# Order of the tap matmuls in a state-space mixer: by tile size instead of group by group

## The chip, the cores and the metric

The kernel runs on one core of one Trainium2 chip. The metric is the device time of one execution in microseconds (us). Three executions of the kernel before took 2615.53, 2616.75 and 2618.24 us; the median, 2616.75 us, is the time before.

## What is computed

Six layers work on x, 256 tokens of 1024 channels in float32. Layers of four kinds of mixer (Fourier, state-space, dilated attention, and a last block with a selective-state and a sparse-attention part) alternate with feed-forward layers (`ffn`). Only the second mixer, the state-space one, is touched. Cut to what matters:

```python
lam_bar = exp(lam * dt)                               # [2 directions, 64 groups, 64 states], complex
b_bar = ((lam_bar - 1) / lam)[..., None] * b          # [.., 64 states, 16 channels]
h[t] = lam_bar * h[t-1] + b_bar @ u[t]                # a scan over 256 tokens, per group, both directions
y[t] = real(c @ h[t])                                 # 16 channels of each group
```

The kernel does this in chunks of 8 tokens. Within a chunk, the output takes the inputs of the same chunk through 16x16 matrices, the taps K_t = Re(C a^t B_bar) for t = -7..7. The taps depend on parameters only, not on x.

## The kernel before, in words

**Dense products.** Nearly all the time is dense products. Weights come in slabs of 128x1024 float32 (512 KB, `W._dma`, L157, on SyncE's queue into 4 buffers). ScalarE makes a rounded copy `whi` (L169), VectorE the remainder `wlo` (L170), into 4 buffers each; two slabs are split ahead of the one in use. `slab_step` issues 12 matmuls for a slab: four times the three products hi*hi, hi*lo and lo*hi (`product`, L307 to L309), with 512 moving columns each.

**Side work.** After every second group of three matmuls `S.tick()` lets the deferred tasks run that are due. So the order of every engine's instructions is fixed when the program is written; each engine takes its own in that order.

**The state-space parameters.** They are prepared while the first feed-forward layer runs. Each weight split calls `s5.run(RATE)`, which puts up small VectorE jobs (`product_jobs`: `first` L1453, `second` L1459 twice, `third` L1464) by a budget of 2.6 units a split. They form the table C a^t for a set of 4 groups in one half of the tile `s5set`. `store` sends that half to DRAM from GpSimd's queue (L1487) and defers `taps(m, ...)` by three ticks. There are 16 sets (m = 0..15); the work for set m+2 writes the half that set m used.

**Taps (L1541 to L1566).** For one set, two PSUM banks `fwd` and `bwd` are filled by small float32 matmuls (L1555). The array is addressed in tiles by `tile_position=(lo, 32 * q)`: q = 0..3 is the group in the set and the quadrant of 32 array columns; `lo` and the height give the array rows. Per part r (real, imaginary) and per q there are three matmuls: `bwd` on rows 64 to 127 (112 moving columns), `fwd` for t = 0 on all 128 rows (16 columns), and `fwd` for t > 0 on rows 0 to 63 (112 columns). That makes 24 matmuls a set; in the trace each shows as two passes, that is two weight loads and two matmuls. After them a matmul with the identity adds the skip term (L1558, two passes), ScalarE copies both banks out (L1563, L1564), and every second set goes to DRAM (L1566). The order of the loops is r, then q, then the three kinds.

**Other tiled matmuls of this kernel**, which the prediction reads as a comparison: `part` (L1752) issues 128-row, 32-column tiles over the four quadrants one after the other; `index_scores` (L907) issues 64-row tiles of all 128 columns for rows 0 and 64 in turn, into two banks; `spread` (L1619) issues 32-row transposes for four row positions in turn, into four banks; `trans` (L476) issues plain 128x128 transposes.

Of the kernel before, what the change touches and what calls it, by code (L numbers as in the profile page):

```python
# [72 lines left out]
class Sched:  # L73
    """Deferred pieces of work, emitted between the steps of the dense products."""
# [12 lines left out]
    def pipeline(self, n, stages, every, wait=0):  # L87
        """stages of (fn, lag): fn(i) at step i + lag; the tasks of the steps"""
        def step(s):
            def f():  # L90
                for fn, lag in sorted(stages, key=lambda x: -x[1]):
                    if 0 <= s - lag < n:
                        fn(s - lag)
            return f
        return self.pace([step(s) for s in range(n + stages[-1][1])], every, wait)

    def join(self, n, fn, delay):
        """defers fn at the n-th call"""
        left = [n]

        def arrive():
            left[0] -= 1
            if left[0] == 0:
                self.defer(fn, delay)
        return arrive
# [20 lines left out]
    def require_in(self, tasks, k):  # L126
        """the same for a task that may only be put up by another one"""
        while k in tasks and tasks[k] is None:
            self._run(self._next())
        if k in tasks:  # L130
            self.require(tasks[k])
# [6 lines left out]
class Weights:  # L138
    """The weight slabs of the whole program in the order of use: DMA, then the
    exact split w = hi + lo, both ahead of the products."""  # L140
# [45 lines left out]
    def split_ahead(self):  # L186
        """one more slab than the products need now"""
        if self.n_split < self.n_used + self.split_bufs:
            self._split()
# [10 lines left out]
class Pair:  # L200
    """An operand in its two exact parts."""
# [6 lines left out]
def tile_two_blocks(ctx: ExitStack, tc: tile.TileContext, A, out, upto=None, taps=None):  # L208
# [96 lines left out]
    def product(ps, lhs, rhs, start, stop):  # L305
        """ps += lhs^T rhs from the exact parts of both."""
        nc.tensor.matmul(ps, lhs.hi, rhs.hi, start=start, stop=False, skip_group_check=True)  # L307
        nc.tensor.matmul(ps, lhs.hi, rhs.lo, start=False, stop=False, skip_group_check=True)  # L308
        nc.tensor.matmul(ps, lhs.lo, rhs.hi, start=False, stop=stop, skip_group_check=True)  # L309

    def rsqrt_steps(v, n):
        """v^-1/2 by Newton's steps from the exponent's estimate: the result and what computes it"""
        y = small.tile([P, n], F32, tag=f"rs{n}", name="rsq")
        t = small.tile([P, n], F32, tag=f"rt{n}", name="rst")

        def estimate():
            nc.vector.tensor_scalar(t.bitcast(I32), v.bitcast(I32), 1, None, OP.logical_shift_right)
            nc.vector.tensor_scalar(y.bitcast(I32), t.bitcast(I32), -1.0, 1597463007.0, OP.mult, OP.add)

        def newton():  # L320
            nc.vector.tensor_tensor(t, y, y, OP.mult)
            nc.vector.scalar_tensor_tensor(t, t, -0.5, v, OP.mult, OP.mult)
            nc.vector.scalar_tensor_tensor(y, t, 1.5, y, OP.add, OP.mult)

        return y, (estimate, newton, newton, newton)
# [7 lines left out]
    class Normed:  # L333
        """x * gain, transposed and split, with the row scale apart."""
# [64 lines left out]
        def chunk_by_parity(self, kc, t):  # L399
            """128 tokens of one parity: the odd ones for t = 0"""  # L400
            S.require(self.tasks[kc // 4])
            s = slice(kc * T + 1 - t, (kc + 1) * T, 2)
            return Pair(self.hi[:, s], self.lo[:, s])
# [10 lines left out]
    def in_proj(xn, nblk, evict, src=None, after_head=None, bank=lambda b: acc()):  # L414
        """natural-layout blocks of 512 columns of (x gain) @ W, each handed to evict."""
        head = {}
        for b, s in order_in(nblk):
            if b not in head:
                head[b] = [bank(b) for _ in range(NT)]
            slab_step(head[b], src(b) if src else xn.chunk, 2 * s, W.take(), s == 0, s == 3)  # L420
            if s == 3:
                evict(b, head.pop(b))
                if b == 1 and after_head is not None:
                    after_head()

    def out_proj(src, nk, scale, xn):
        """x += scale * (y @ W); the halves of the next norm start as they end."""
        for h in range(2):
            ps = [acc() for _ in range(NT)]
            for s in range(nk // 2):  # L430
                slab_step(ps, src, 2 * s, W.take(), s == 0, s == nk // 2 - 1)
            for t in range(NT):
                xs = x[:, t, h * 512:(h + 1) * 512]
                nc.vector.scalar_tensor_tensor(xs, ps[t], scale, xs, OP.mult, OP.add)  # L434
            xn.half_ready(h)

    class Chunks:
        """A transposed operand [k, tokens] in two parts, 128 rows a chunk."""
# [86 lines left out]
    def bias_vectors():  # L525
        """The additive score term of every head by offset, in DRAM as [head, 512 | 256 | 256]:
        one group of heads per part, a large negative where the offset is not attended."""
# [23 lines left out]
    def backwards(ap):  # L551
        """[p, 256 tokens] read at 255 - t - 2 n for (t, n)"""
# [4 lines left out]
    def attention(xn, nxt):  # L557
# [16 lines left out]
        def unit_block(b):  # L574
            """block -> (half, unit or None, group)"""
# [190 lines left out]
    def sincos(ang, sin, cos, t):  # L766
        """sin and cos of ang; t is scratch of the same shape, ang is lost"""
# [10 lines left out]
    def rope_tables():  # L778
        """per rotated width n: cos [p, t, n] and (-sin, sin) [p, t, 2, n]"""
# [16 lines left out]
    def rope(v, t, first, n):  # L796
        """v [p, heads, width] rotated in place in its first 2n columns"""
# [13 lines left out]
    def transposed(src, widths=128):  # L811
        """[p, 128] tiles, one per entry of src, transposed side by side into one bank"""
# [5 lines left out]
    def mixer(xn, nxt, li):  # L818
# [76 lines left out]
        def index_scores(t, h0):  # L895
            """the scores of queries t, from heads h0 on as many as two banks hold"""
# [32 lines left out]
        def top_keys(i):  # L929
            """8 more of the 64 best keys of each query"""  # L930
# [81 lines left out]
        def steps():  # L1012
            """dt = softplus, and the running sum of dt a"""
# [59 lines left out]
        def similar():  # L1073
            """C B^T per group, causal, then the heads one by one"""
# [60 lines left out]
        def normalize(g):  # L1135
            """the gate and the norm of a group of 8 heads, then its four chunks of 128 channels"""
# [137 lines left out]
    class S5:  # L1274
        """The state-space mixer in chunks of 8 tokens: the groups' inputs of a chunk reach the state at its
        end (the other end for the backward direction) through B_bar a^k, the state runs over the 32 chunks,
        and a chunk's outputs take C a^k of the state before it and the taps K_t = Re(C a^t B_bar) of the
        tokens in it. Groups go in sets of 4 (one per partition quadrant), channels as (direction, state)."""
# [21 lines left out]
        def plan(self):  # L1300
# [128 lines left out]
            def sums(side, part):  # L1429
                """for products of x in three multiplications: x0 + x1 and y0 + y1, y0 - y1"""  # L1430
# [12 lines left out]
            def product_jobs(side, m):  # L1443
                """(q, r, (j, k)) of 4 groups: x times the conjugate of y for side c, times y for side b"""
# [96 lines left out]
        def taps(self, m, ct):  # L1541
            """K of a set of 4 groups to DRAM: columns are bwd t = 7..1, t = 0, fwd t = 1..7"""
# [3 lines left out]
            ct = ct.rearrange("p (q r k) -> p q r k", q=4, r=2)  # L1546
            for r in range(2):
                for q in range(4):
                    g = 4 * m + q
                    n = 16 if q == 3 else 32  # L1550
                    lhs = bb[:, r, g:g + n // 16].rearrange("p g k -> p (g k)")
                    for ps, at, lo, hi, rhs in ((bwd, 0, 64, 128, ct[64:, q, r, 16:]),
                                                (fwd, 0, 0, 128, c[:, r, g]),
                                                (fwd, 16, 0, 64, ct[:64, q, r, :112])):
                        nc.tensor.matmul(ps[32 * q:32 * q + n, at:at + rhs.shape[1]], lhs[lo:hi], rhs,  # L1555
                                         start=r == 0 and at == 0, stop=r == 1, skip_group_check=True,
                                         tile_position=(lo, 32 * q))
# [19 lines left out]
        def first_half(self, xn):  # L1577
            """the first half of the channels, without the row scale, while the products before go on"""
# [12 lines left out]
        def turn_in(self, xn, h, e):  # L1591
            """x to U's order [(j, p), chunk]: 4 pieces of 2 chunks of 128 channels each"""
# [42 lines left out]
        def mix(self, xn, nxt):  # L1635
# [44 lines left out]
            def place(k):  # L1680
                """the chunk ends of two sets, transposed, to the order of the steps"""
# [31 lines left out]
            def scan_ops(w):  # L1713
                """the steps of one half of the groups, op by op; each ends with the copies it lets go"""
# [88 lines left out]
        def outputs(self, b, ps, oT):  # L1803
            """the steps from the sums of two chunks of 128 channels to their part of the operand"""
# [233 lines left out]
```

## Time and profile before

| what | value |
| --- | --- |
| median of three executions | 2616.75 us |
| span of the profiled execution, first to last instruction | 2613.9 us |
| TensorE busy | 2529.4 us, 97% of the span, 13056 matmul passes |
| VectorE busy | 1617.6 us, 62% |
| ScalarE busy | 1338.9 us, 51% |
| stretch with the taps, 80 to 235 us: TensorE / VectorE / ScalarE busy | 155.0 / 98.0 / 48.9 us |
| share of L1555 in the chain of that stretch | 41.8% |

The execution that was profiled has no time of its own beside its span; the span is 2.85 us below the median. "PE" is TensorE's matmuls, "PEld" its weight loads, DVE is VectorE, ACT ScalarE, POOL GpSimd, SP SyncE. Shapes such as 64\*32 are the rows and columns of the array tile; 64x112 is partitions by moving columns. In the timelines neighbouring instructions of one line are merged: a row gives the start of the first, the time to the end of the last, and their number. A matmul's duration includes its way through the array, so durations of neighbours overlap.

### The profile page before, as it was taken

To read this page: it belongs to the slowest core of one execution; us is meant where nothing else is said; L and a number is where in the kernel's file an instruction comes from. 1 tells how busy PE (TensorE), PEld (TensorE's weight loads), DVE (VectorE), ACT (ScalarE), POOL (GpSimd) and SP (SyncE) were. 2 spreads that over 40 slices of the span, in tenths; PEclk is the share of its full clock that TensorE was granted. 3 is DMA by queue.
4 is the path that set the end of the run, shared out by engine and by line. 5 is a ranking of instruction groups with operands and counts; after the bars stand their busy time and mean duration, and the time that the engine had idled before them with its cause. 6 is when DMAs were issued, how large, how long until landed. Compare 5 with 4: busy or idle time off the path is not lost.

```text
span 2613.9 us, 34796 instructions
## 1 busy us (share of the span) xinstructions
PE 2529.4 (97%) x13056; PEld 2069.1 (79%) x13056; DVE 1617.6 (62%) x2870; ACT 1338.9 (51%) x2053; POOL 56.4 (2%) x98
## 2 busy tenths in 40 slices
PE   8999969999999999999999999899999999999998
PEld 6767747888778888888888888788888888778886
DVE  7757876555565556555555556776555555876654
ACT  5334565544455555444444445675444444676543
POOL 0000000000100100000000000000000000000000
PEclk9999989999999999999999999999999999999999
DMA  5545696555644525645555565545565655545554
GB/s 178 179 161 182 211 231 219 183 184 163 212 157 129 164 96 178 193 146 171 184 180 194 184 192 160 171 130 166 187 193 178 190 188 175 173 132 163 178 182 148
DMA packets 131945, 456.35 MB, mean 175 GB/s; under 512 B 14889, under 2 KB 23988, under 8 KB 129344
## 3 DMA queue, kind: packets, MB, share of 16 engines
q1 hardware_dynamic: 123616, 426.96, 51.4%
q0 software_dynamic: 7584, 26.51, 3.1%
q8 instruction: 103, 1.69, 0.3%
q10 hardware_dynamic: 576, 0.66, 0.1%
q14 instruction: 66, 0.54, 0.1%
HBM read 437.57 MB, written 16.50 MB: 174 GB/s over the span
## 4 chain that ended last, share of the span: by engine, by line
PE 59%; issue 32%; DVE 3%; DMA 3%; ACT 3%; POOL 0%; ACTq 0%; SPq 0%; DVEq 0%; POOLq 0%
PE acc L307 17%; PE acc L309 16%; PE acc L308 16%; PE aux L1555 2%; PE aux L815 1%; DMA local<-s_k 1%; PE aux L476 1%; DVE wlo L170 1%; ACT whi L169 1%; PE aux L674 1%; DMA csb<-cs_d 1%; PE aux L715 0%; DMA raw<-in_qkv_dram 0%; PE aux L381 0%; PE aux L1211 0%
## 5 line engine op out<-in xcount | busy, mean ns | idle before, releaser
L170 DVE TENSOR_TENSOR wlo<-raw,whi 128x1024 fp32r<-128x1024 f32 (+1 forms) x774 | 922.9, 1219 | 420.8 <-ACT whi L169 419.3
L169 ACT ACTIVATE whi<-raw 128x1024 fp32r<-128x1024 f32 (+1 forms) x774 | 790.3, 1054 | 266.1 <-PE acc L309 234.3
L307 PE MATMUL acc<-whi,xhi 128*128 128x512 f32 (+1 forms) x2104 | 845.8, 402 | 5.6 <-ACT whi L169 3.1
L308 PE MATMUL acc<-wlo,xhi 128*128 128x512 f32 (+1 forms) x2104 | 822.2, 391 | 5.4 <-DVE wlo L170 5.1
L309 PE MATMUL acc<-whi,xlo 128*128 128x512 f32 (+1 forms) x2104 | 823.4, 391 | 0.0
L307 PEld LDWEIGHTS acc<-whi,xhi 128*128 128x128 f32 x2104 | 398.4, 189 | 89.1 <-issue 6.2
L308 PEld LDWEIGHTS acc<-wlo,xhi 128*128 128x128 f32 x2104 | 398.9, 190 | 83.4 <-DVE wlo L170 8.1
L309 PEld LDWEIGHTS acc<-whi,xlo 128*128 128x128 f32 x2104 | 397.7, 189 | 84.9
L307 PE MATMUL acc<-whi,yhi 128*128 128x512 f32 x976 | 387.4, 397 | 2.1 <-ACT yhi L451 1.1
L308 PE MATMUL acc<-wlo,yhi 128*128 128x512 f32 x976 | 381.5, 391 | 3.2 <-DVE wlo L170 3.2
L309 PE MATMUL acc<-whi,ylo 128*128 128x512 f32 x976 | 381.6, 391 | 0.0
L468 ACT ACTIVATE silu<-acc,rsq 128x256 f32<-128x256 f32 x176 | 83.4, 474 | 289.0 <-PE acc L309 289.0
L469 DVE SCALAR_TENSOR_TENSOR hb<-acc,rsq,silu 128x256 f32<-128x256 f32 x176 | 84.7, 483 | 228.5 <-ACT silu L468 228.4
L308 PEld LDWEIGHTS acc<-wlo,yhi 128*128 128x128 f32 x976 | 183.9, 188 | 40.9 <-DVE wlo L170 4.4
L307 PEld LDWEIGHTS acc<-whi,yhi 128*128 128x128 f32 x976 | 183.8, 188 | 40.4 <-ACT yhi L741 1.6
L309 PEld LDWEIGHTS acc<-whi,ylo 128*128 128x128 f32 x976 | 183.6, 188 | 39.9 <-DVE ylo L452 0.7
L451 ACT ACTIVATE yhi<-aux 128x512 fp32r<-128x512 f32 (+1 forms) x104 | 58.7, 564 | 192.6 <-PE aux L476 190.1
L452 DVE TENSOR_TENSOR ylo<-aux,yhi 128x512 fp32r<-128x512 f32 (+1 forms) x104 | 67.5, 649 | 105.8 <-ACT yhi L451 105.5
L390 ACT ACTIVATE xhi<-aux,gains 128x256 fp32r<-128x256 f32 x104 | 40.7, 475 | 86.3 <-PE aux L381 86.3
L392 DVE SCALAR_TENSOR_TENSOR xlo<-aux,gains,xhi 128x256 fp32r<-128x256 f32 x104 | 43.1, 478 | 50.6 <-ACT xhi L390 50.6
L434 DVE SCALAR_TENSOR_TENSOR x<-acc,x 128x512 f32<-128x512 f32 x52 | 35.7, 692 | 56.3 <-PE acc L309 56.3
L1555 PE MATMUL aux<-s5set,s5bb 64*32 64x112 f32 (+1 forms) x512 | 54.5, 266 | 0.0
(359 smaller groups left out, 1942.0 us busy)
## 6 DMA issues: line engine op xcount, KB each, us to landing
raw<-in_ffn_in_dram SPq DMA_DIRECT2D x352, 512.0 KB, 4.2
raw<-in_ffn_out_dram SPq DMA_DIRECT2D x176, 512.0 KB, 4.1
raw<-in_mix_in_dram SPq DMA_DIRECT2D x96, 512.0 KB, 3.6
raw<-in_qkv_dram SPq DMA_DIRECT2D x72, 512.0 KB, 4.3
raw<-in_mix_out_dram SPq DMA_DIRECT2D x32, 512.0 KB, 3.6
raw<-in_fnet_w_out_dram SPq DMA_DIRECT2D x16, 512.0 KB, 3.9
s_ct<-s5set POOLq DMA_DIRECT2D x16, 512.0 KB, 3.8
raw<-in_s_glu_dram SPq DMA_DIRECT2D x16, 512.0 KB, 4.5
```

The lines of the kernel that those rows point to most:

```text
L169: self.nc.scalar.activation(hi[:, :w], r, AF.Copy)
L170: self.nc.vector.tensor_tensor(lo[:, :w], r, hi[:, :w].bitcast(F32), OP.subtract)
L307: nc.tensor.matmul(ps, lhs.hi, rhs.hi, start=start, stop=False, skip_group_check=True)
L308: nc.tensor.matmul(ps, lhs.hi, rhs.lo, start=False, stop=False, skip_group_check=True)
L309: nc.tensor.matmul(ps, lhs.lo, rhs.hi, start=False, stop=stop, skip_group_check=True)
L390: nc.scalar.activation(hi, p, AF.Copy, scale=g)
L392: nc.vector.scalar_tensor_tensor(lo, p, g, hi.bitcast(F32), OP.mult, OP.subtract)
L451: nc.scalar.activation(p.hi, ps, AF.Copy)
L452: nc.vector.tensor_tensor(p.lo, ps, p.hi.bitcast(F32), OP.subtract)
L468: nc.scalar.activation(s, ps[t][:, :256], AF.Silu, scale=r)
L469: nc.vector.scalar_tensor_tensor(hb[:, t * 256:(t + 1) * 256], ps[t][:, 256:], r, s, OP.mult, OP.mult)
L1555: nc.tensor.matmul(ps[32 * q:32 * q + n, at:at + rhs.shape[1]], lhs[lo:hi], rhs, start=r == 0 and at == 0, stop=r == 1, skip_group_check=True,
```

## The change

Inside `taps` the body of the innermost loop becomes a function `step`, and the calls of it are put in another order: first the eight 128-row matmuls of the set over r and q, then the sixteen 64-row ones, rows 64 to 127 and rows 0 to 63 in turn, over r and q. The matmuls, their operands, their tiles and their start and stop flags are the same, as is all that follows. Elsewhere the diff only takes out comment strings, which issue nothing.

```diff
+            def step(ps, at, r, q, lo, hi, rhs):
+                g = 4 * m + q
+                n = 16 if q == 3 else 32
+                lhs = bb[:, r, g:g + n // 16].rearrange("p g k -> p (g k)")
+                nc.tensor.matmul(ps[32 * q:32 * q + n, at:at + rhs.shape[1]], lhs[lo:hi], rhs,
+                                 start=r == 0 and at == 0, stop=r == 1, skip_group_check=True,
+                                 tile_position=(lo, 32 * q))
+
             for r in range(2):
                 for q in range(4):
-                    g = 4 * m + q
-                    n = 16 if q == 3 else 32
-                    lhs = bb[:, r, g:g + n // 16].rearrange("p g k -> p (g k)")
-                    for ps, at, lo, hi, rhs in ((bwd, 0, 64, 128, ct[64:, q, r, 16:]),
-                                                (fwd, 0, 0, 128, c[:, r, g]),
-                                                (fwd, 16, 0, 64, ct[:64, q, r, :112])):
-                        nc.tensor.matmul(ps[32 * q:32 * q + n, at:at + rhs.shape[1]], lhs[lo:hi], rhs,
-                                         start=r == 0 and at == 0, stop=r == 1, skip_group_check=True,
-                                         tile_position=(lo, 32 * q))
+                    step(fwd, 0, r, q, 0, 128, c[:, r, 4 * m + q])
+            for r in range(2):
+                for q in range(4):
+                    step(bwd, 0, r, q, 64, 128, ct[64:, q, r, 16:])
+                    step(fwd, 16, r, q, 0, 64, ct[:64, q, r, :112])
             nc.tensor.matmul(fwd[:112, :16], ident[:, :112], self.skip[:, m * 16:(m + 1) * 16],
                              start=False, stop=True, skip_group_check=True)
```

## Rows read from the trace of the kernel before

**Rows 1.** The page: span, and busy time of each engine.
```profile
span 2613.9 us, 34796 instructions
...
PE 2529.4 (97%) x13056; PEld 2069.1 (79%) x13056; DVE 1617.6 (62%) x2870; ACT 1338.9 (51%) x2053; POOL 56.4 (2%) x98
```

**Rows 2.** Busy time by stretch: the taps, the rest of the preparation, the mixer.
```profile
core 0: us, PE busy (x) PEld busy (x) DVE busy (x) ACT busy (x) POOL busy (x), PEclk, DMA share, GB/s
80.00:235.00 155.00, 155.00 (x1186) 107.86 (x1185) 98.02 (x120) 48.85 (x85) 14.16 (x24) 1.00 0.52 173
235.00:275.00 40.00, 40.00 (x204) 33.44 (x203) 36.83 (x46) 21.45 (x31) 4.88 (x10) 1.00 0.66 215
...
380.00:420.00 40.00, 26.18 (x373) 20.02 (x374) 23.54 (x104) 25.52 (x36) 1.58 (x3) 0.82 0.79 256
```

**Rows 3.** Chain of 80 to 235 us: start, length, engine and line.
```profile
by line: PE aux L1555 41.8%; PE acc L307 18.3%; PE acc L308 17.4%; PE acc L309 17.3%; PE aux L1558 3.1%; PE aux L476 2.3%
...
81.17 4.05 PE aux L1555 x46
...
85.84 0.23 PE acc L308
...
229.41 4.05 PE aux L1555 x46
```

**Rows 4.** Timeline of TensorE in one set of taps (start, length, instructions).
```profile
160.03 0.38 PE L1555 MATMUL aux<-s5set,s5bb 64*32 64x112 f32 x2
160.34 0.24 PE L1555 MATMUL aux<-s5c,s5bb 128*32 128x16 f32 x2
160.50 0.38 PE L1555 MATMUL aux<-s5set,s5bb 64*32 64x112 f32 x4
160.82 0.23 PE L1555 MATMUL aux<-s5c,s5bb 128*32 128x16 f32 x2
160.98 0.38 PE L1555 MATMUL aux<-s5set,s5bb 64*32 64x112 f32 x4
...
164.08 0.37 PE L1558 MATMUL aux<-s5skip,ident 128*112 128x16 f32 x2
```

**Rows 5.** Timeline of 160.81 to 160.83 us alone: the second passes.
```profile
160.62 0.26 PE L1555 MATMUL aux<-s5set,s5bb 64*32 64x112 f32 x2
```

**Rows 6.** Timeline of the quadrant matmuls of the mixer.
```profile
397.06 1.08 PE L1752 MATMUL acc<-ct,H 128*32 128x128 f32 x32 [1.41 <-DMA ct<-s_ct]
...
412.72 3.27 PE L1752 MATMUL acc<-local,H 128*32 128x128 f32 x112 [0.58 <-ACT H L1735]
```

**Rows 7.** Timeline of the two-row-half matmuls of the last block.
```profile
1630.93 1.14 PE L907 MATMUL aux<-kiT,qiT 64*128 64x256 f32 x8
```

**Rows 8.** Timeline of the transposes at four row positions.
```profile
356.41 0.69 PE L1619 MATMUL acc<-ident,hq 32*128 32x32 f32 x32
```

**Rows 9.** Chain of 88 to 89 us: four plain transposes of 128 columns.
```profile
88.37 0.44 PE aux L476 x4
```

**Rows 10.** Busy time and granted clock around rows 6 and rows 7.
```profile
397.05:398.20 1.15, 1.08 (x32) 0.81 (x32) 0.37 (x2) 1.12 (x3) 0.29 (x1) 1.00 0.96 399
1630.90:1632.00 1.10, 1.10 (x10) 0.70 (x9) 1.10 (x4) 0.00 (x0) 0.00 (x0) 1.00 0.84 331
```

**Rows 11.** Timeline of VectorE, 159 to 183 us: idle times in brackets.
```profile
165.75 1.23 DVE L170 TENSOR_TENSOR wlo<-raw,whi 128x1024 fp32r<-128x1024 f32 x1 [1.51 <-ACT whi L169]
...
175.06 0.48 DVE L469 SCALAR_TENSOR_TENSOR hb<-acc,rsq,silu 128x256 f32<-128x256 f32 x1 [3.89 <-ACT silu L468]
...
176.37 0.48 DVE L469 SCALAR_TENSOR_TENSOR hb<-acc,rsq,silu 128x256 f32<-128x256 f32 x1 [0.83 <-ACT silu L468]
177.32 1.22 DVE L170 TENSOR_TENSOR wlo<-raw,whi 128x1024 fp32r<-128x1024 f32 x1 [0.47 <-ACT whi L169]
```

**Rows 12.** Waits of 80 to 235 us: total us, times, longest.
```profile
ACT taps L1563 <- PE aux L1555: 69.7, 16, 6.6
DVE wlo L170 <- ACT whi L169: 32.1, 18, 4.4
```

## The prediction

> **What bounds the kernel now.** I read the page first, for the engine that fills the span: TensorE is busy 97% of 2613.9 us, VectorE 62% [rows 1]. That is an average, so next I cut the span where the changed line runs. Its 16 sets lie between 81.17 and 229.41 + 4.05 = 233.46 us [rows 3], and in 80 to 235 us TensorE is busy 155.0 of 155 us at full granted clock, VectorE 98.0, ScalarE 48.9, with the DMA engines half used [rows 2]. The chain of that stretch is TensorE alone: 41.8% of it is L1555, the rest dense products [rows 3]. So a microsecond taken from the taps is a microsecond of the kernel, as long as TensorE stays the last to be ready. One set holds the chain for 4.05 us, the first as the last [rows 3]; 16 x 4.05 = 64.8 us is all that there is to gain.
>
> Then I asked what those 4.05 us are. The timeline of a set shows a beat: four 64-row passes from 160.50, two 128-row passes from 160.82, and the next 64-row ones from 160.98 [rows 4]. That is 0.32 + 0.16 = 0.48 us per (r, q), eight times, 3.8 us, and the ends make 4.05. What streams in a beat is little. A plain pass of 128 columns takes 0.44 / 4 = 0.11 us [rows 9], so one of 112 columns takes 0.096. In the 0.32 us two tiles run side by side, two passes each: 0.19 us. The second passes start at 160.62 [rows 5], so they have streamed by 160.72, and yet the next tile size starts only at 160.82: 0.10 us in which the array empties. The same 0.10 out of the 128-row part's 0.16 leaves 0.06 for its two passes of 16 columns, 0.03 each, mostly their weight loads. So a set pays about 0.10 us sixteen times for a change of tile size, and lets at most two of its tiles work at once.
>
> **The change, part by part.** Removed: the alternation of tile sizes. A set now changes size once inside (128 to 64 rows), and once to the skip matmul, which it did before too. Added: nothing; 48 passes stay 48. Moved: order within one set on one engine's queue, so nothing is moved past a DMA, SP's or POOL's instructions. The wait for `s5set` moves from the first matmul to the ninth, which can only be earlier ready; no wait is added.
>
> *Part one, eight 128-row matmuls over four quadrants.* The trace has the like: L1752, 128 rows by 32 columns over the quadrants. 32 passes of 128 columns take 1.08 us there and 112 take 3.27 [rows 6], at full clock [rows 10]: with the last one's way through the array in it, 3.27 / 112 = 0.029 us a pass, against 0.11 alone [rows 9]. Four quadrants work at once, without loss. So part one is four rounds (two r, two passes) of about 0.03 us, 0.02 for the start of the other quadrants, and 0.10 to empty: 0.24 us. Bounds: 0.16, one old 128-row part; and 8 x 0.06 + 0.10 = 0.58, if quadrants didn't overlap. I take 0.24, since L1752 is the nearest row.
>
> *Part two, sixteen 64-row matmuls.* Eight tiles (four quadrants, two row halves). That both halves of one column strip work at once is shown by L907: 8 passes of 256 columns take 1.14 us to the end of the last [rows 7], at full clock [rows 10], where one after another at 0.22 each would need 1.76. Eight tiles at once are shown nowhere. If they all work together, it is four rounds of 0.096 us, 0.03 for the first weights, 0.05 for the start of the others, 0.10 to empty: 0.56 us. If only four do, it is eight rounds: 0.95. If only the pairs of the present order do, 16 rounds and 1.7. I take 0.56: quadrants and row halves are each free in the trace, and no row shows a limit on both.
>
> Sum: 0.24 + 0.56 = 0.80 us a set for 4.05. 16 x 3.25 = 52 us. The profiled execution's 2613.9 us would become 2561.9; the median lies 2.85 above that span, so 2616.75 - 52 = 2564.75, say 2565 us.
>
> *Is it kept?* Once TensorE needs only 155 - 52 = 103 us here, VectorE with 98.0 is next: 95%. What it waits for is ScalarE (wlo after whi, 32.1 us), and ScalarE in turn stands 69.7 us before the copies of the taps, that is, behind TensorE [rows 12]. So those waits shrink with the taps. Those that stay between two sets and the next two are 1.51, 0.83 and 0.47 us [rows 11]; they exist only while VectorE is early, and vanish when it is late. The weights are split two slabs ahead, 2 x 12 x 0.23 = 5.5 us of dense work [rows 3], which covers one late set. I therefore cost VectorE at nothing; without that cover see the fourth rival. ScalarE goes to 48.9 of 103, the DMA engines from 0.52 to 0.52 x 155 / 103 = 0.78, which the mixer's own stretch reaches too (0.79) [rows 2]. The next stretch, 235 to 275 us, is in TensorE's hands with VectorE at 92% [rows 2]; it starts from the last taps as before, so what is won stays won.
>
> **A rule against it.** In rows 6, passes on four quadrants of the same array rows follow each other at 0.029 us, so their weight loads are hidden. The Trainium skill ("TensorE: Matmul & The Clock Gate", Part 3, "The mechanism") says that a weight load overlaps with matmuls in flight only when its row group differs, which the quadrants of a half don't do. By that rule the passes of a half would follow each other; the fifth rival is priced for that mechanism, from rows. L1752 speaks against it.
>
> Also, 32 passes of 32 columns take 0.69 us elsewhere [rows 8], 0.022 each. The Trainium skill ("TensorEngine Tiling (Array Packing)", Performance Considerations, "Instruction Overhead") states some 60 cycles for each matmul however short; by that figure sixteen passes in line would make part one 16 x 0.025 + 0.10 = 0.50 us, an estimate from that page, and the time 4 us more. These passes are quicker, with their tail in it.
>
> **The rivals.**
> 1. *Half the tiles at once.* Rows 7 show two row halves, rows 6 four quadrants, no row eight tiles. Part two 0.95: set 1.19, gain 16 x 2.86 = 46 us: 2571.
> 2. *Feeding.* 96 weight loads and matmuls would leave the queue in 0.8 us. The longest run of small passes that I read, 112 in 3.27 us [rows 6], is 0.029 a pass, though streaming bounds it; 48 x 0.029 + 0.10 = 1.49, gain 16 x 2.56 = 41: 2576. Against it: the passes at 0.022 [rows 8].
> 3. *No effect.* The engine reorders passes over tiles already, or a later stage gives the gain back. Against it: the beat of rows 4 repeats through every set, and the later mixer waits follow program order. 2617.
> 4. *VectorE takes over.* If the waits of rows 11 (2.81 us per two sets) stay in full, two sets take 98.0 / 8 + 2.81 = 15.1 us against 12.9 for TensorE, so 2.2 x 8 = 17 us are lost: 2582. For it: 95% load. Against it: those waits go when it runs late.
> 5. *Loads in line.* Part one 16 x 0.03 + 0.10 = 0.58; part two, each half's 16 passes at 0.12 (0.03 load, 0.096 stream): 2.0. Gain 16 x 1.45 = 23: 2594.
> 6. *Slower: tiles next to each other that drain.* If going from one row half to the other in the same column strip empties the array, as a change of size does, each 64-row matmul costs what the lone first one does, 0.31 us (160.03 to 160.34) [rows 4]: 16 x 0.31 + 8 x 0.16 = 6.2 us a set, +2.2 x 16 = 35: 2652. It decides from 4.05 / 24 = 0.17 us a matmul. Against it: rows 7, where the halves alternate in one strip and overlap.
>
> **How the numbers follow.** Forecast 0.58; rivals 1 to 6: 0.12, 0.09, 0.04, 0.11, 0.03, 0.03. Faster by over 0.2% (5 us, about what three runs can tell from no change): forecast and rivals 1, 2, 4, 5, 0.93; within: 0.04; slower: 0.03. Low end: part one at 0.16 and no start costs in part two (0.51) make 0.67 a set, 54 us, 2563, and some us below for the mixer stage, whose granted clock of 0.82 [rows 2] depends on where its idle times fall: 2559. High end: rivals 1, 2 and 4 in: 2583. Left out: about 0.1 above, and little below.
>
> **What would show it.** In the profile after, a set from its first matmul to the skip matmul: 0.8 us (right), 1.2 (rival 1), 1.5 with gaps (rival 2), 2.6 (rival 5), over 4 (rival 6); and one change of tile size in it, not sixteen. TensorE busy through a stretch that is 52 us shorter; idle TensorE there, with wlo or `s5set` as releaser, would show rival 4. L1752's stretch should stay as long as it is. The prediction is wrong if the set shrinks and the stretch doesn't, or if the set stays over 1.6 us.

## The result, and the profile after

The kernel after takes 2569.4 us (median of 4 runs, 2566.44 to 2571.25) against 2616.49 us for the kernel before (4 runs beside it): ratio 0.9817, 95% interval 0.9802 to 0.9831, 47.1 us faster. The forecast was 2565 us, range 2559 to 2583. The execution that was profiled took 2569.61 us, with a span of 2567.8.

The page after, span and busy time; they answer to [rows 1].

```profile
span 2567.8 us, 34798 instructions
...
PE 2480.4 (97%) x13056; PEld 2044.3 (80%) x13056; DVE 1615.8 (63%) x2870; ACT 1338.3 (52%) x2053; POOL 56.4 (2%) x98
```

The same 13056 passes, and 49 us less of TensorE busy: the work is the same, it only overlaps more. Next comes one set of taps of the kernel after on TensorE, which answers to [rows 4] (the line is L1551 now, the skip matmul L1562).

```profile
121.08 0.31 PE L1551 MATMUL aux<-s5c,s5bb 128*32 128x16 f32 x16
121.32 0.60 PE L1551 MATMUL aux<-s5set,s5bb 64*32 64x112 f32 x32
121.85 0.37 PE L1562 MATMUL aux<-s5skip,ident 128*112 128x16 f32 x2
122.07 0.48 PE L307 MATMUL acc<-whi,xhi 128*128 128x512 f32 x1
```

Two rows where there were seventeen: sixteen 128-row passes, then 0.24 us later thirty-two 64-row passes, and 0.53 us later the skip matmul. That is 0.77 us where it was 4.05, and by the starts in the trace all sixteen sets take 0.77. The chain of 80 to 183 us answers to [rows 3] (first row the shares by line, then one set):

```profile
by line: PE acc L307 27.6%; PE acc L309 26.4%; PE acc L308 26.1%; PE aux L1551 12.0%; PE aux L1562 4.6%; PE aux L476 3.4%
...
82.20 0.77 PE aux L1551 x38
```

Busy time of the stretch with the taps, and of the one behind it, as in [rows 2]:

```profile
80.00:183.00 103.00, 103.00 (x1188) 81.33 (x1187) 96.14 (x120) 48.35 (x85) 13.67 (x24) 1.00 0.79 256
183.00:223.00 40.00, 40.00 (x204) 33.45 (x203) 37.47 (x47) 21.46 (x31) 5.06 (x10) 1.00 0.70 223
```

TensorE is busy for all of 103 us at full granted clock: VectorE, at 96.14 of 103 (93%), never holds it up. And the waits of the two engines beside it, which answer to [rows 12], shrank with the taps instead of staying:

```profile
ACT taps L1567 <- PE aux L1551: 25.6, 15, 3.9
...
DVE wlo L170 <- ACT whi L169: 2.9, 6, 0.7
```

So where did the time go? From the first weight load of the first set to the first dense matmul behind the last set, the trace before has 152.52 us (81.10 to 233.62), the one after 100.00 (82.13 to 182.13): 52.5 us less. The span is 46.1 us shorter. The other 6.4 came back: 1.0 ahead of the first set, 0.6 between the taps and the mixer stage and 5.5 in the mixer stage, less 0.7 in the rest. That stage, before:

```profile
340.79 0.39 PE L309 MATMUL acc<-whi,ylo 128*128 128x512 f32 x1
...
371.11 1.93 PE L1752 MATMUL acc<-local,U 128*32 128x128 f32 x32 [3.64 <-DMA local<-s_k]
377.36 1.93 PE L1752 MATMUL acc<-local,U 128*32 128x128 f32 x32 [4.31 <-DMA local<-s_k]
...
399.57 1.08 PE L1752 MATMUL acc<-ct,H 128*32 128x128 f32 x32 [1.42 <-DMA ct<-s_ct]
400.58 0.50 PE L307 MATMUL acc<-whi,yhi 128*128 128x512 f32 x1
```

and after:

```profile
289.93 0.39 PE L309 MATMUL acc<-whi,ylo 128*128 128x512 f32 x1
...
322.32 1.94 PE L1756 MATMUL acc<-local,U 128*32 128x128 f32 x32 [2.84 <-issue]
329.83 1.94 PE L1756 MATMUL acc<-local,U 128*32 128x128 f32 x32 [5.58 <-DMA local<-s_k]
...
354.21 1.08 PE L1756 MATMUL acc<-ct,H 128*32 128x128 f32 x32 [1.04 <-DMA ct<-s_ct]
355.23 0.50 PE L307 MATMUL acc<-whi,yhi 128*128 128x512 f32 x1
```

The stage took 59.8 us before and 65.3 after. In brackets stands the idle time of TensorE ahead of a row, and what ended it: mostly the transfer of the taps into `local`, and at the end that of the table `ct`, which SyncE issues behind it. The matmuls on `local` are as long in both. TensorE was busy for longer in the stage as a whole, though, at a lower mean granted clock (busy time, as in [rows 2]; first before, then after, then a further profile of the kernel after, the run after_third below):

```profile
340.79:400.58 59.79, 31.14 (x461) 20.84 (x459) 43.10 (x195) 38.71 (x52) 1.88 (x6) 0.77 1.04 270
...
289.93:355.23 65.30, 35.26 (x461) 23.68 (x459) 43.11 (x195) 37.62 (x51) 1.61 (x6) 0.66 1.06 253
...
288.51:348.82 60.31, 35.31 (x461) 23.70 (x459) 42.97 (x195) 37.54 (x50) 1.36 (x5) 0.66 1.06 269
```

The last row shows that this does not set the length of the stage: 35.31 us busy at 0.66, and a stage of 60.3. The experiments ask two things: which part of the change made the 52.5 us, and whether the loss in the mixer stage belongs to the change.

### The profile page after: what moved, and what is told of

It reads as the page before. It is cut to its first block, busy times and chain, and to the rows that moved or that the text cites. A ratio compares the mean times of both kernels' runs of the same rounds, so it can differ in the third digit from the quotient of the medians.

```text
span 2567.8 us, 34798 instructions
## 1 busy us (share of the span) xinstructions
PE 2480.4 (97%) x13056; PEld 2044.3 (80%) x13056; DVE 1615.8 (63%) x2870; ACT 1338.3 (52%) x2053; POOL 56.4 (2%) x98
## 3 DMA queue, kind: packets, MB, share of 16 engines
q1 hardware_dynamic: 123616, 426.96, 52.7%
## 4 chain that ended last, share of the span: by engine, by line
PE 66%; issue 24%; DVE 3%; DMA 3%; ACT 2%; POOL 0%; SPq 0%; ACTq 0%; DVEq 0%; POOLq 0%
PE acc L307 20%; PE acc L308 19%; PE acc L309 19%; DMA local<-s_k 1%; PE aux L674 1%; PE aux L476 1%; PE aux L815 1%; PE aux L715 1%; DVE wlo L170 1%; PE aux L381 1%; ACT whi L169 1%; DMA raw<-in_qkv_dram 1%; PE aux L699 1%; PE aux L1551 0%; DMA ct<-s_ct 0%
## 5 line engine op out<-in xcount | busy, mean ns | idle before, releaser
L476 PEld LDWEIGHTS aux<-ident,hb 128*128 128x128 f32 x352 | 44.0, 140 | 11.2
```

Of the source, the lines that this page charges most:

```text
L476: nc.tensor.transpose(pt[:, u * T + t * P:u * T + (t + 1) * P], hb[:, t * 256 + u * P:t * 256 + (u + 1) * P], ident)
```

## The experiments

In each profile I read four numbers. The *stretch* is the one above (first weight load of the taps to the first dense matmul behind the last set). The *stage* is the mixer stage, from the last dense matmul ahead of it to the first behind it. The *gather* is the time from the first to the last of the 8192 packets of 512 bytes that bring the taps back from DRAM into `local`, by the trace's DMA records. *Behind* is the time from the end of the stage to the end of the span. The ratio is to the kernel before run beside it. The runs before_again, after_again, qmajor and alt shared one chip; halves, skipq and the two plain ones a second; after_third, halves_again and skipq_again a third.

| run | median us | ratio (95% interval) | stretch | stage | gather | behind |
| --- | --- | --- | --- | --- | --- | --- |
| before, first profile | 2616.49 | 1 | 152.5 | 59.8 | 28.7 | 2213.4 |
| before_again | 2612.38 | 0.9995 (0.9985 to 1.0004) | 152.5 | 61.4 | 29.9 | 2212.8 |
| after, first profile | 2569.4 | 0.9817 (0.9802 to 0.9831) | 100.0 | 65.3 | 32.9 | 2212.6 |
| after_again | 2566.64 | 0.9823 (0.9809 to 0.9838) | 100.0 | 66.5 | 34.2 | 2209.9 |
| after_third | 2560.79 | 0.9792 (0.9779 to 0.9806) | 100.0 | 60.3 | 29.0 | 2211.1 |
| qmajor | 2562.15 | 0.9807 (0.9789 to 0.9826) | 102.2 | 63.3 | 32.0 | 2204.1 |
| alt | 2567.31 | 0.9822 (0.9803 to 0.9841) | 104.6 | 63.5 | 31.6 | 2210.5 |
| halves | 2560.19 | 0.9795 (0.9779 to 0.9810) | 100.4 | 59.6 | 28.4 | 2214.0 |
| halves_again | 2560.0 | 0.9794 (0.9780 to 0.9807) | 100.3 | 62.1 | 31.4 | 2207.1 |
| skipq | 2554.49 | 0.9772 (0.9757 to 0.9786) | 97.5 | 63.3 | 30.8 | 2203.4 |
| skipq_again | 2557.23 | 0.9777 (0.9764 to 0.9790) | 97.5 | 62.2 | 29.6 | 2202.0 |
| plain_before | 2606.26 | 0.9971 (0.9959 to 0.9982) | 152.5 | 60.2 | none | 2202.4 |
| plain_after | 2552.87 | 0.9766 (0.9748 to 0.9784) | 100.0 | 60.2 | none | 2201.7 |

The last column scatters by 12 us, more than the stage does, between kernels that issue the same work there. Part of it lies in single waits for transfers: in the last block ScalarE waits 7.0 us for `csb` in the first profile after and 1.5 us in skipq. So medians that lie a few us apart do not rank these orders. The stretch does: it repeats to 0.1 us from profile to profile of one kernel.

**qmajor: grouped by size, one quadrant after the other.**

```diff
-            for r in range(2):
-                for q in range(4):
+            for q in range(4):
+                for r in range(2):
                     step(fwd, 0, r, q, 0, 128, c[:, r, 4 * m + q])
-            for r in range(2):
-                for q in range(4):
-                    step(bwd, 0, r, q, 64, 128, ct[64:, q, r, 16:])
-                    step(fwd, 16, r, q, 0, 64, ct[:64, q, r, :112])
+            for q in range(4):
+                for r in range(2):
+                    step(bwd, 0, r, q, 64, 128, ct[64:, q, r, 16:])
+                for r in range(2):
+                    step(fwd, 16, r, q, 0, 64, ct[:64, q, r, :112])
```

> Grouped by tile size as in the kernel after, but within a size one quadrant after the other: per q both parts r, and in the 64-row part rows 64 to 127 for both r, then rows 0 to 63. This keeps the one change of size and takes away the neighbours on other tiles. Theory 1 (the change of size is what cost; the array takes passes past those that wait for a busy tile): a set stays at 0.8 us to 1.0, time within 4 us of the kernel after. Theory 2 (passes start in program order, so neighbours must be on other tiles): part one 16 x 0.03 + 0.1 = 0.6, part two at most two tiles at once, 16 rounds of 0.096 = 1.6: 2.2 us a set, 23 us slower than the kernel after, 2592.

TensorE's timeline of one set of qmajor:

```profile
120.77 0.33 PE L1551 MATMUL aux<-s5c,s5bb 128*32 128x16 f32 x16
121.02 0.70 PE L1551 MATMUL aux<-s5set,s5bb 64*32 64x112 f32 x32
121.65 0.37 PE L1563 MATMUL aux<-s5skip,ident 128*112 128x16 f32 x2
```

0.88 us, as theory 1 had it. Now four passes for one tile stand next to each other in program order, and the array still works on the tiles side by side: passes for free tiles start ahead of earlier ones that wait for a busy tile. The trace shows it directly: the tile of the fourth quadrant is last in program order and the only one of 16 columns (64\*16); its first 64-row pass starts at 121.13, 0.11 us into part two, while passes of the other three quadrants go on starting until 121.41. So what stands in the section on the kernel before, that each engine takes its instructions in the order written, does not hold for TensorE's passes on different tiles. The order over the quadrants is worth 0.11 us a set, 2.2 us in the stretch (102.2 against 100.0). The other 50 us come from the order by size.

The median does not show those 2.2 us: qmajor took 2562.15 us, 4.5 us less than after_again beside it. In the profiles its stage was 3.2 us shorter and the part behind it 5.8 us shorter, which lies within the scatter of both.

**alt: the sizes alternate once per part r.**

```diff
             for r in range(2):
                 for q in range(4):
                     step(fwd, 0, r, q, 0, 128, c[:, r, 4 * m + q])
-            for r in range(2):
                 for q in range(4):
                     step(bwd, 0, r, q, 64, 128, ct[64:, q, r, 16:])
                     step(fwd, 16, r, q, 0, 64, ct[:64, q, r, :112])
```

> The order over quadrants and row halves of the kernel after, but once per part r: four 128-row matmuls, eight 64-row ones, and again. Three changes of size inside a set where the kernel after has one. Theory 1 (a change of size costs the emptying of the array, 0.1 us, and the start of the first pass anew): 2 x 0.18 + 2 x 0.34 = 1.05 us a set, +0.28, 4.5 us slower than the kernel after. Theory 2 (the gain came from tiles side by side alone, the change of size being free once four are in flight): 0.77, no difference.

One set of alt on TensorE:

```profile
122.39 0.25 PE L1551 MATMUL aux<-s5c,s5bb 128*32 128x16 f32 x8
122.57 0.41 PE L1551 MATMUL aux<-s5set,s5bb 64*32 64x112 f32 x16
122.91 0.25 PE L1551 MATMUL aux<-s5c,s5bb 128*32 128x16 f32 x8
123.09 0.41 PE L1551 MATMUL aux<-s5set,s5bb 64*32 64x112 f32 x16
123.43 0.37 PE L1561 MATMUL aux<-s5skip,ident 128*112 128x16 f32 x2
```

0.18 + 0.34, twice: 1.04 us, where 1.05 was expected. The same 48 passes, two more changes of size, and 0.27 us more a set (4.6 us in the stretch), about 0.14 for each change. Theory 2 is out: with four and eight tiles at work a change of size is still paid. At this price the fifteen changes that a set has fewer (one inside it for sixteen) are about 2.0 of the 3.28 us saved, an estimate; the rest would be more tiles at work at once. No run parts the two.

**halves: rows 64 to 127 first, then rows 0 to 63.**

```diff
             for r in range(2):
                 for q in range(4):
                     step(bwd, 0, r, q, 64, 128, ct[64:, q, r, 16:])
+            for r in range(2):
+                for q in range(4):
                     step(fwd, 16, r, q, 0, 64, ct[:64, q, r, :112])
```

> The kernel after, with the 64-row matmuls in two runs: all eight on rows 64 to 127, then all eight on rows 0 to 63. Theory 1 (passes go past those that wait for a busy tile, as far as some tens of them): the second half starts beside the first, set 0.77 to 0.85 us to the skip matmul. Theory 2 (a half must have started all its passes before the other begins): four rounds of 0.096 us, then four more, less what the start of the last round overlaps: 0.24 + 0.03 + 7 x 0.096 + 0.05 + 0.10 = 1.1 us, 5 us slower in the stretch.

One set of halves on TensorE:

```profile
126.73 0.31 PE L1551 MATMUL aux<-s5c,s5bb 128*32 128x16 f32 x16
126.97 0.63 PE L1551 MATMUL aux<-s5set,s5bb 64*32 64x112 f32 x32
127.54 0.37 PE L1564 MATMUL aux<-s5skip,ident 128*112 128x16 f32 x2
```

0.81 us: theory 1. In the trace the 64-row passes start in groups of four, two groups every 0.10 to 0.12 us, where one half alone, at 0.096 us of streaming a pass, could start one group. So the second half's passes run beside the first half's, ahead of those that still wait.

**before_again, after_again: no edit, second profiles.**

> The kernel before, unchanged, profiled a second time. Of the 52.5 us that the stretch of the taps lost, some 6 us came back in the mixer stage, from the last dense matmul ahead of the L815 transposes to the first one behind L1752: it took 59.8 us in the first profile before (340.79 to 400.58) and 65.3 in the one after (289.93 to 355.23). Theory A (that stage differs between executions of one kernel: pace of the 512-byte gather of the taps, and where the granted clock falls): it scatters here too, by 2 us or more from 59.8. Theory B (the new order makes that stage longer): 59.8 within 1 us here. Both: time ratio 1.000.

> The kernel after, unchanged, profiled a second time. Theory A (the mixer stage differs between executions of one kernel): it lies anywhere in 59 to 66 us, and a short one comes with a time near 2564. Theory B (the new order makes it longer): 65 us within 1 again, and 2569 again. Both: the sixteen sets 0.77 us each, as in the first profile.

The sets kept their lengths to 0.01 us, but neither theory on the mixer stage came off: the kernel before moved by 1.6 us, less than A asked, and the kernel after by 1.2, more than B allowed but still at the long end. The time was 47.4 us below the kernel before again, so at this point the change itself was still a suspect.

**plain_before, plain_after: without the gather.** The edit is the same in both.

```diff
             t = big(F32, "local")
-            kd = self.kd.rearrange("m (q k) x -> k (m q) x", q=4)
-            for j in range(8):
-                nc.sync.dma_start(t[16 * j:16 * j + 16].rearrange("p (g x) -> p g x", g=16),
-                                  kd[:16, 16 * i:16 * i + 16, (7 - j) * 16:(7 - j) * 16 + 128])
+            nc.sync.dma_start(t, self.ct_d[i])
             return t
```

> The kernel before with the gather of the taps left out: the four tiles `local` are loaded whole from the table beside it (one 1 MB transfer of 8 KB packets each) and not in 512-byte pieces from the taps' tensor; so the chunk-local part of the output is left wrong, and the matmuls that read it do the same work. This is the reference for plain_after. The gather ran 28.7 and 29.9 us in the two profiles before; 4 MB in large packets should take about 10. Mixer stage 59.8 to 61.4 us -> about 42, time about 2595. Theory A and theory B: the same here.

> The kernel after with the same gather left out. In the four profiles with the taps grouped by size the mixer stage took 63.3 to 66.5 us and the gather 31.6 to 34.2, in the two before 59.8 to 61.4 and 28.7 to 29.9. Theory A (what came back there is the pace of the 512-byte packets and the granted clock beside them, which differ between executions): without the gather the stage takes the same time in both orders within 1 us, and the whole gain of 52.5 us shows: plain_before less plain_after 51 to 54. Theory B (something else in that stage got longer by the order, or by arriving there earlier): the difference stays at 47 to 48, and the stage 4 to 5 us longer than in plain_before.

Both leave the taps out of the output, which is therefore not the right one; the matmuls are the same. The difference of the medians is 2606.26 - 2552.87 = 53.4 us, and the stage takes 60.2 us in both. That is theory A's number: without the gather the whole gain is in the time. But the stage did not shrink to 42 us as I had expected of both, and plain_before took 2606 us and not 2595. What it gained on the kernel before lies behind the stage (2202.4 against 2213.4 us in the profiles), where skipq has 2203.4 with the gather. TensorE's timeline of plain_after shows why the stage stayed:

```profile
318.72 4.87 PE L1753 MATMUL acc<-local,U 128*32 128x128 f32 x128
342.56 1.08 PE L1753 MATMUL acc<-ct,H 128*32 128x128 f32 x16 [18.97 <-ACT H L1736]
343.82 5.51 PE L1753 MATMUL acc<-ct,H 128*32 128x128 f32 x112 [0.18 <-ACT H L1736]
349.29 0.50 PE L307 MATMUL acc<-whi,yhi 128*128 128x512 f32 x1
```

The `local` matmuls now run in one go, and then TensorE waits 18.97 us for `H`, the states that ScalarE copies out of VectorE's scan. That comes 53.4 us into the stage. The scan ran beside the gather all the time; taking the gather away only made the scan the last to arrive. The three profiles with the shortest gathers (28.4 to 29.0 us) have stages of 59.6 to 60.3 us, as if there were none; the others, from 29.6 us up, have 61.4 to 66.5. So the gather costs time where it takes longer than about 29 us.

**after_third, halves_again: no edit, to settle whether the loss belongs to the order.**

> The kernel after, unchanged, a third time. So far its two profiles had the longest mixer stages (65.3 and 66.5 us; gather 32.9 and 34.2) and its times lay 47.1 and 47.4 us below the kernel before, while halves, with a stretch of the taps as short, had 59.6, 28.4 and 52.5. Theory A (the gather's pace differs between executions, whatever the order): a third profile can have a stage of 59 to 66 us; the ratio of the times settles between 0.979 and 0.983. Theory C (this very order of the 64-row matmuls makes the later stage longer, halves does not): stage 65 to 66.5 again, 47 us below again, and halves_again at 52.

> The kernel with the two 64-row halves one after the other, a second time. Theory A: the mixer stage lies anywhere in 59 to 66 us, here too; time 47 to 53 us below the kernel before. Theory C (this order spares the later stage): 59.6 within 1 again, 52 us below again, 4 to 5 us faster than after_third.

The mixer stage of the kernel after, third profile:

```profile
318.67 1.94 PE L1756 MATMUL acc<-local,U 128*32 128x128 f32 x32 [1.07 <-issue]
325.08 1.93 PE L1756 MATMUL acc<-local,U 128*32 128x128 f32 x32 [4.48 <-DMA local<-s_k]
331.34 1.93 PE L1756 MATMUL acc<-local,U 128*32 128x128 f32 x32 [4.32 <-DMA local<-s_k]
...
341.20 1.08 PE L1756 MATMUL acc<-ct,H 128*32 128x128 f32 x16 [1.05 <-ACT H L1739]
...
348.82 0.50 PE L307 MATMUL acc<-whi,yhi 128*128 128x512 f32 x1
```

The matmuls on `local` start 6.4 and 6.3 us apart here, 7.5 and 6.6 apart in the first profile, and TensorE already waits for `H`, 52.7 us into the stage. The stage is 60.3 us, the time 2560.79, 53.4 us below the kernel before; halves_again has 62.1 us of stage and is 0.8 us below after_third, not 4 to 5. Theory C is out. One and the same kernel shows a stage of 60.3 and of 66.5, and over the eleven profiles that have a gather the stage grows with it, by and large: from 28.4 and 59.6 to 34.2 and 66.5. So the change need not make the stage longer. That it does so on average is not excluded: the two profiles of the kernel before have 59.8 and 61.4 us, the nine of the others 59.6 to 66.5. Nor are executions told apart from chips: the stage of 66.5 and that of 60.3 come from two chips.

**skipq, skipq_again: the skip term on the quadrants, between the two sizes.**

```diff
+            for q in range(4):
+                n = 16 if q == 3 else 32
+                nc.tensor.matmul(fwd[32 * q:32 * q + n, :16], ident[:, 32 * q:32 * q + n],
+                                 self.skip[:, m * 16:(m + 1) * 16], start=False, stop=True,
+                                 skip_group_check=True, tile_position=(0, 32 * q))
             for r in range(2):
                 for q in range(4):
                     step(bwd, 0, r, q, 64, 128, ct[64:, q, r, 16:])
                     step(fwd, 16, r, q, 0, 64, ct[:64, q, r, :112])
-            nc.tensor.matmul(fwd[:112, :16], ident[:, :112], self.skip[:, m * 16:(m + 1) * 16],
-                             start=False, stop=True, skip_group_check=True)
```

> The kernel after, with the skip term as four matmuls of 32 columns over the quadrants behind the 128-row ones, in place of one full matmul behind the 64-row ones. One change of tile size fewer, and two passes a quadrant more in part one. If a pass in part one costs its weight load alone (0.027 us), part one grows by 0.055 and the 0.22 of the full matmul go: a set to the next dense matmul 0.99 -> 0.83 us, 2.5 us faster than the kernel after in the stretch of the taps (100.0 -> 97.5). If four more matmuls start one after the other: 8 x 0.03 = 0.24 and no gain.

> The version with the skip term on the quadrants, a second time, to see whether it stays the fastest. By the stretch of the taps (97.5 us against 100.0 and 152.5) it should lie 2.5 us below the kernel after and 55.0 below the one before; 58.2 were measured. Theory A: 53 to 58 below.

One set of skipq on TensorE:

```profile
125.59 0.31 PE L1551 MATMUL aux<-s5c,s5bb 128*32 128x16 f32 x16
125.73 0.24 PE L1560 MATMUL aux<-s5skip,ident 128*16 128x16 f32 x8
125.90 0.60 PE L1551 MATMUL aux<-s5set,s5bb 64*32 64x112 f32 x32
126.43 0.50 PE L307 MATMUL acc<-whi,xhi 128*128 128x512 f32 x1
```

0.84 us to the next dense matmul, where the kernel after has 0.99 (121.08 to 122.07). The eight passes of the skip term stretch the 128-row part from 0.24 to 0.31, and the 0.22 of the full matmul are gone. The stretch is 97.5 us, 2.5 shorter than in the kernel after, as expected. In time it is 3.6 us faster than after_third on the same chip (2557.23 against 2560.79); the two intervals against the kernel before overlap, so by time alone that is not certain. The 2.5 us of the stretch are, and they are all that the edit is shown to give. The two medians of skipq lie 58.2 and 57.0 us below the kernel before, where the stretch gives 55.0, and the profiles of skipq_again and after_third differ by 9 us behind the stage as well.

## Why the prediction was right

- *What a set costs.* Predicted 0.24 + 0.56 = 0.80 us, measured 0.24 + 0.53 = 0.77. The rounds were right: eight tiles do work at once, which no row before had shown. In the set shown above the passes of part two start in four rounds of eight, 0.12, 0.10 and 0.10 us apart. Part two was 0.03 too dear: the first weights, the start of the other tiles and the emptying came to about 0.02, 0.03 and 0.09 us, by the starts in the trace and 0.096 us of streaming a pass, where the sum had 0.03, 0.05 and 0.10.
- *What the sets save.* Predicted 52 us, measured 52.5 in every profile of this order.
- *Whether it is kept.* VectorE was costed at nothing, and that held at 93% load, and its waits, behind ScalarE's wait for the taps, shrank with it: from 32.1 and 69.7 us [rows 12] to 2.9 and 25.6.
- *The term that was off.* The forecast had the mixer stage stay as long as it is, and gave its scatter only to the low end of the range. In the profiled execution the stage took 5.5 us more, which is about what 2565 missed 2569.4 by (4.4 us). The stage is bound by the 512-byte gather once that takes over about 29 us; the gather took 28.7 and 29.9 us in the two profiles before and 28.4 to 34.2 in the nine others. In a further run of the same kernel, after_third, the gain was 53.4 us.
- *What was luck.* The forecast took all that follows the mixer stage to be as long as before. It differed by only 0.7 us between the two first profiles, but by up to 12 us over all thirteen. So the 52.5 us of the stretch bear the prediction out; that the median came within 5 us of the forecast is in part luck.
- *The rivals.* Half the tiles at once: no, part two is 0.53 us. Feeding: no, 48 passes start in 0.77 us. No effect: no. VectorE: no, TensorE has no idle time in the stretch. Loads in line: no; part one's sixteen passes take 0.24 us, the emptying included, where that rival had 0.58. Beside it the prediction put a rule of the Trainium skill ("TensorE: Matmul & The Clock Gate", Part 3, "The mechanism"), that a weight load overlaps with matmuls in flight only when its row group differs; these sixteen passes on the same rows do not agree with it. Draining between neighbours: no; the row halves alternate in part two. Rival 3 held one true thing that I had not expected: the engine does take passes past those that wait (qmajor). A change of tile size it did not hide: alt paid 0.14 us for each.

What stays open: why the packets of the gather take 57 ns on average in one profile and 71 in another of kernels that do the same there; whether the order, the chip or neither has a part in it; and what makes the part behind the stage scatter. None of it was tried.

## What to carry to other kernels

When small tiled matmuls of different tile sizes alternate, sort them by size before anything else: each change costs about 0.14 us here, and between two changes the order before had at most two tiles at work. The order within a size matters little: the two others tried cost 0.04 and 0.11 us a set of 0.77. And before a loss elsewhere is put down to a change, profile the same kernel again: two profiles of one kernel differed here by more than the whole error of the forecast.

## What the runs showed of the hardware that was not expected

- Thirty-two passes on eight tiles, written one tile after the other (qmajor) or one half after the other (halves), still overlap: 0.63 and 0.57 us for the 64-row part against 0.53 in the best order. In qmajor a pass of the last quadrant starts 0.11 us into the part, ahead of passes that stand before it in the program.
- Eight tiles of 64 rows by 32 columns, two row halves on four quadrants, stream at once without slowing each other: 32 passes of 112 columns in 0.53 us, the emptying included.
- The stage that the gather seemed to bind (TensorE waits 12.1 us there for `local` in the first profile before) took 60.2 us when the gather was taken out, against 59.8 and 61.4 with it.
